# A hybrid encoder layer: the output norm of cross attention with its roots on ScalarE and VectorE, later first-half rows, other PSUM banks and five early FFN pairs

## The chip, the cores and the metric

The kernel runs on one core of one Trainium2 chip. The core has five engines with a queue each, worked off in order: TensorE (PE, matmuls and transposes), VectorE (DVE), ScalarE (ACT), GpSimd (POOL) and SyncE (SP), whose queue issues the DMAs here. The metric is the device time of one execution in microseconds (us).

## The reference

One layer of an encoder trunk in float32, for 1024 tokens of width 1024. Three sub-layers follow each other, each inside two RMS norms, one ahead of it and one on its output before it is added to the residual stream:

```python
c = _memory_cross_attention(_rms_norm(x, g_cross_pre[l]), _rms_norm(mem, g_mem[l]),
                            w_cq[l], w_ckv[l], w_co[l])
x = x + _rms_norm(c, g_cross_post[l])
f = _swiglu(_rms_norm(x, g_ffn_pre[l]), w_gate_up[l], w_down[l])
x = x + _rms_norm(f, g_ffn_post[l])
```

`_rms_norm(x, g)` is `x * rsqrt(mean(x*x) + EPS) * g` along a row, `_swiglu` is `(silu(h @ w_gate) * (h @ w_up)) @ w_down` with 2816 columns each for gate and up. The mixer ahead of this (attention and a delta rule) is not touched.

## The kernel before, in words

Every float32 product is made of three matmuls: each operand is split into a high part `hi` (a cast on ACT) and a low part `lo` (the difference, on DVE or POOL), and hi·hi, hi·lo and lo·hi are summed in PSUM. `split` (line 100) issues the two instructions (lines 103 and 104, or 106 and 107 where a gain is multiplied in). `load_w` (line 119) brings a weight matrix of 128x1024 into one of two buffers `wraw`, and splits it into one of two pairs `whi`, `wlo`. A `wraw` buffer is free again when its `lo` has been computed, a `whi`, `wlo` pair when its last matmul has run.

The stretch around the change comes in this order:

1. The output projection of cross attention (lines 1277 to 1412) is a Strassen-like product of 2x2 blocks. Its last two products are issued by tile of 128 rows (`by_tile`, line 1385), on four PSUM banks `X`, two of the pool `PN` and two of `PX`. After each tile `then(t)` follows: `second_rows(t)` for rows 4 to 7 of eight (tokens 512 to 1023, tensor `zl`), and in the last product `first_half_rows(t)` for rows 0 to 3 (tensor `zz`).
2. `row_end` (line 1391) and `finish` (line 1308) end a row: square and sum its second half (ACT), multiply by the gain `gp` (`gained`), the reciprocal root of the mean square, scale and add the residual (line 1315), store to `d_x2` (line 1316), then square and sum again (line 1318), a second reciprocal root (lines 161 and 162), and scale for the FFN's input norm (line 1322 on ACT for even rows, line 1324 on DVE for odd rows). Each root is `(s + c)` to the power -0.5 on POOL, line 1314 or 162.
3. The rows are turned. `turned_k` (line 1418) makes four transposes of 128x128 into one bank. The eight blocks `k` of rows 4 to 7 come first (line 1430), each split into `x1h`, `x1l`; blocks 0 to 3 are the operand `X11`, blocks 4 to 7 `X21`. Then the blocks of rows 0 to 3 are turned, and combined with the first into `T1` to `T4` and `X22` (lines 1438 to 1455), mostly on DVE.
4. The FFN's gate and up matrices are worked in 11 pairs of 256 columns. For the first `EARLY` pairs (loop at line 1474) the products with `X11` and `X21`, which need only rows 4 to 7, are made ahead, while rows 0 to 3 and `T1` to `T4` still come into being: for each of two matrices 12 matmuls with `X11`, a copy to `d_m1` (line 1483), 12 matmuls with `X21`, then SiLU (line 1487), a product (line 1488) and a store to `d_a`. That is 48 matmuls to a pair, on four banks `PG`, two to a pair.
5. The main loop (line 1564) takes all 11 pairs, early and other pairs in turn. `pair_weights` (line 1507) loads each pair's matrices (for early pairs a second time), sums their blocks on POOL and DVE (lines 1516 to 1519) and splits the sums. An early pair reads `d_m1` and `d_a` back and has 48 matmuls fewer here. The first matmuls are `pB`, with `T2`.

What sets the order: the program is traced as written, and a scheduler then lays out each engine's queue with a simulation of time; of what is ready in that simulation, what was traced first goes first. `tc.high_priority(AHEAD)` counts an instruction as traced 300 earlier. `tc.issue_after(i)` puts the instructions of its block that run on `i`'s engine behind `i` in that engine's queue; it adds no wait and binds no other engine.

Of the kernel before, what the change touches and what calls it, by code (L numbers as in the profile page):

```python
# [10 lines left out]
F32 = mybir.dt.float32  # L11
F32R = mybir.dt.float32r
I32 = mybir.dt.int32
AF = mybir.ActivationFunctionType
ALU = mybir.AluOpType
# [4 lines left out]
P = 128  # L20
S = 1024
D = 1024
# [4 lines left out]
EPS = 1e-6  # L27
# [1 line left out]
AHEAD = 300  # L29
ML = 256  # L30

EARLY = 4

# [41 lines left out]
def tile_hybrid_block(  # L77
# [6 lines left out]
    nc = tc.nc  # L84
# [9 lines left out]
    def f32(ap):  # L94
        return ap.bitcast(F32)
# [4 lines left out]
    def split(hi, lo, src, scale=None, eng=None):  # L100

        if scale is None:
            nc.scalar.copy(hi, src)  # L103
            (eng or nc.vector).tensor_tensor(lo, src, f32(hi), ALU.subtract)  # L104
        else:
            nc.scalar.activation(hi, src, AF.Identity, scale=scale)
            nc.vector.scalar_tensor_tensor(lo, src, scale, f32(hi), ALU.mult, ALU.subtract)

    def pool(name, bufs, **kw):
        return tc.tile_pool(name=name, bufs=bufs, reuse_waits="tile", **kw)  # L110

    cst = ctx.enter_context(pool("cst", 1))
# [20 lines left out]
    ident = cst.tile([P, P], F32, name="ident")  # L133
    mhalf = cst.tile([P, 16], F32, name="mhalf")
    nc.gpsimd.memset(mhalf, -0.5)
    cols = cst.tile([P, P], F32, name="cols")
    p12 = ExitStack()
    sm = p12.enter_context(pool("sm", 1))
# [19 lines left out]
    def rstd_of(rs, ss, n, eps):  # L158

        w = ss.shape[-1]  # L160
        nc.gpsimd.tensor_scalar(rs, ss, n, eps, ALU.mult, ALU.add)
        nc.gpsimd.tensor_tensor(rs, rs, mhalf[:, :w], ALU.pow)
# [5 lines left out]
    def gain(n, k):  # L168
        return cols[:, gain_at[n] + k:gain_at[n] + k + 1]
# [28 lines left out]
    def small():  # L198
        return ps.tile([P, 512], F32, tag="ps", name="ps")
# [11 lines left out]
    for hf in range(2):  # L211
        hi = hx.tile([P, KT, HALF], F32R, name=f"hhi{hf}")
        lo = hx.tile([P, KT, HALF], F32R, name=f"hlo{hf}")
        for j in range(4):
            t = 4 * hf + j
# [4 lines left out]
            ss = t1.tile([P, 1], F32, tag="ss", name="ss", bufs=4)  # L220
            nc.scalar.activation(junk, xt, AF.Square, accum_out=ss)
            rs = t1.tile([P, 1], F32, tag="rs", name="rs", bufs=4)
            rstd_of(rs, ss, 1.0 / D, EPS)
            nc.vector.scalar_tensor_tensor(xt, xt, rs, gmix, ALU.mult, ALU.mult)
            for kq in range(2):
                pt = small()
# [15 lines left out]
    pt = small()  # L242
# [75 lines left out]
    pt = small()  # L318
# [42 lines left out]
    pt = small()  # L361
# [640 lines left out]
    HK = KT // 2  # L1002
# [19 lines left out]
    def operand(pool_, tag):  # L1022
        if tag == "s1":
            return [Halves(opB, b0), Halves(opB3, "b3")]
        if tag == "s0":
            return [Halves(opA, f"s0{c}") for c in "hl"]
        if tag in places:
            return [p_.tile([P, KT, HALF], F32R, tag=t, name=t) for p_, t in places[tag]]
        return [pool_.tile([P, KT, HALF], F32R, tag=f"{tag}{i}", name=f"{tag}{i}") for i in range(2)]
# [20 lines left out]
    PG, PN, PX = (pg, "pg"), (pn, "pn"), (px, "px")  # L1050
# [198 lines left out]
    zl = opC.tile([P, 4, D], F32, tag="x22", name="zl")  # L1249
# [3 lines left out]
    zz = tz.tile([P, 4, D], F32, name="zz")  # L1253
    zv, za = zl[:, :, 0:HALF], zl[:, :, HALF:]
    ssq = tz.tile([P, 2, NT], F32, name="ssq")

    def blocks(t):
        return t[:, 0:HK], t[:, HK:KT]
# [45 lines left out]
    def square_of(src, ch, r):  # L1304
        jk = tz.tile([P, HALF], F32, tag="junk", name="junk")
        nc.scalar.activation(jk, src, AF.Square, accum_out=ssq[:, ch, r:r + 1])

    def finish(r, z, eng):

        tok = slice(r * P, (r + 1) * P)  # L1310
        xr = res[r]
        rs = tz.tile([P, 1], F32, tag="prs", name="prs", bufs=4)
        nc.vector.tensor_scalar(rs, ssq[:, 1, r:r + 1], ssq[:, 0, r:r + 1], D * EPS, ALU.add, ALU.add)
        nc.gpsimd.tensor_tensor(rs, rs, mhalf[:, 0:1], ALU.pow)
        nc.vector.scalar_tensor_tensor(xr, z, rs, xr, ALU.mult, ALU.add)
        nc.sync.dma_start(d_x2[tok, :], xr)
        s2 = tz.tile([P, 1], F32, tag="ps2", name="ps2", bufs=4)
        nc.scalar.activation(z, xr, AF.Square, accum_out=s2)
        r2 = tz.tile([P, 1], F32, tag="pr2", name="pr2", bufs=4)
        rstd_of(r2, s2, 1.0 / D, EPS)  # L1320
        if eng is nc.scalar:
            nc.scalar.activation(z, xr, AF.Identity, scale=r2)
        else:
            nc.vector.tensor_scalar(z, xr, r2, None, ALU.mult)

    a11, a12, s3_, a22 = ((q_[0][:, c], q_[1][:, c]) for q_ in (q0, q1) for c in (slice(0, HK), slice(HK, KT)))
    s1_, s4_ = ([r_, [t[:, c] for t in q1]] for r_, c in zip(blocks(raw), (slice(HK, KT), slice(0, HK))))
# [4 lines left out]
    def add(o_, a, b_):  # L1332
        nc.vector.tensor_tensor(o_, a, b_, ALU.add)

    def gained(o_, src, c_, eng=nc.gpsimd):
        eng.tensor_tensor(o_, src, gp[:, c_], ALU.mult)

    LO, HI = slice(0, HALF), slice(HALF, D)
# [22 lines left out]
    for t in range(4):  # L1361
        add(zv[:, t], zv[:, t], X[t])
        square_of(zv[:, t], 0, 4 + t)
        gained(zv[:, t], zv[:, t], LO)

    def residual_row(r, place=None):
        if place is None:
# [23 lines left out]
    def row_end(z, r):  # L1391
        square_of(z[:, HI], 1, r)
        gained(z[:, HI], z[:, HI], HI, nc.vector)
        finish(r, z, (nc.scalar, nc.vector)[r % 2])

    def second_rows(t):
        add(za[:, t], y7[:, t], X[t])
        row_end(zl[:, t], 4 + t)

    def first_half_rows(t):  # L1400
        add(zz[:, t, HI], e_[:, t], X[t])
        row_end(zz[:, t], t)

    by_tile([act_part(s1_, k) for k in (0, 2)], resident(1, ("s0h1", "s0l0")), False, second_rows)
    two_rows(0, "s0h1")
    two_rows(2, "s0h0")
# [8 lines left out]
    x1h, x1l = operand(opB, "s1")  # L1415
    X11, X21 = (x1h[:, 0:HK], x1l[:, 0:HK]), (x1h[:, HK:KT], x1l[:, HK:KT])

    def turned_k(parts, k, at=PN):
        pt = at[0].tile([P, 512], F32, tag=at[1], name="ptn")
        for j in range(4):  # L1420
            nc.tensor.transpose(pt[:, j * P:(j + 1) * P], parts(j, k), ident)
        return pt
# [5 lines left out]
        return zz[:, j, k * P:(k + 1) * P]  # L1428

    for k in range(KT):  # L1430
        pt = turned_k(first_rows, k, (PN, PX)[k % 2])
        split(x1h[:, k, :], x1l[:, k, :], pt, gain("ffn", k))
        nc.gpsimd.tensor_tensor(raw[:, k, :], f32(x1h[:, k, :]), f32(x1l[:, k, :]), ALU.add)
    tr = LR2.enter_context(pool("tr", 1, side="right"))
    T2, T4 = (blocks(t) for t in operand(opA, "s0"))
    T1, T3 = (blocks(t) for t in operand(opB, "s2"))
# [23 lines left out]
    d_a = {n: dram.tile([NB, P, HALF], F32, name=f"d_a{n}") for n in ("11", "12", "22", "s1", "s2", "s3", "s4")}  # L1460
    d_m1 = dram.tile([2 * EARLY, P, HALF], F32, name="d_m1")

# [9 lines left out]
    te = LP.enter_context(pool("te", 2, side="right"))  # L1472
    for e in range(EARLY):
        f = 2 * e
# [31 lines left out]
    def pair_weights(c0, early):  # L1506

        with tc.high_priority(AHEAD):
            raws = []
            for i in range(2):  # L1510
                raws.append(wp.tile([P, KT, P], F32, tag="wraw", name="wraw"))
                load = nc.sync.dma_start(raws[i], w_gate_up[:, c0 + i * P:c0 + (i + 1) * P].rearrange("(k p) n -> p k n", p=P))
            a_, b_ = raws
            s = [ws.tile([P, HK, P], F32, tag="sr", name="sr", bufs=3) for _ in range(4)]
            hl = {i: [ws.tile([P, HK, P], F32R, tag=f"s{i}{c}", name=f"s{i}{c}") for c in "hl"] for i in (1, 0, 2, 3)}
            nc.gpsimd.tensor_tensor(s[0], b_[:, 0:HK], b_[:, HK:], ALU.add)  # L1516
            nc.vector.tensor_tensor(s[1], s[0], a_[:, 0:HK], ALU.subtract)
            nc.gpsimd.tensor_tensor(s[2], a_[:, 0:HK], b_[:, 0:HK], ALU.subtract)
            nc.vector.tensor_tensor(s[3], a_[:, HK:], s[1], ALU.subtract)
            for i in (1, 0, 2, 3):  # L1520
                split(*hl[i], s[i])
            W1 = None
            if not early:
                ahi = wp.tile([P, KT, P], F32R, tag="whi", name="whi")
                alo = wp.tile([P, KT, P], F32R, tag="wlo", name="wlo")
                split(ahi, alo, a_, eng=nc.gpsimd)
                W1 = (ahi[:, 0:HK], alo[:, 0:HK]), (ahi[:, HK:], alo[:, HK:])
            W22 = [tg.tile([P, HK, P], F32R, tag=n, name=n) for n in ("bhi", "blo")]
            split(*W22, b_[:, HK:])
        return W1, W22, [hl[i] for i in range(4)], load  # L1530
# [28 lines left out]

    turns = [p for e in range(EARLY) for p in (e, EARLY + e)] + list(range(2 * EARLY, NB))  # L1560
    for f in (2 * p for p in turns):
        early = f // 2 < EARLY
        wts = [pair_weights(c0, early) for c0 in (f * P, FF + f * P)]
# [35 lines left out]
        s1, s2 = (tg.tile([P, HALF], F32, tag="sa", name="sa") for _ in range(2))  # L1599
# [29 lines left out]
    zz = keep.tile([P, 4, D], F32, name="zz")  # L1629
    za, zv = (keep.tile([P, 4, 512], F32, name=n) for n in ("za", "zv"))  # L1630
# [113 lines left out]
    for t in range(4):  # L1744
# [13 lines left out]
        r = 4 + t  # L1758
        xr = residual(r)
# [4 lines left out]
        rs = rstd_at(r)  # L1764
# [35 lines left out]
```

## Time and profile before

| | |
|---|---|
| median of three runs | 1534.2 us (1531.57 to 1537.82) |
| the profiled execution | 1537.92 us, its span 1536.2 us |
| mean granted TensorE clock | 0.992 |
| DVE busy | 1109.5 us (72%), 1790 instructions |
| ACT busy | 742.3 us (48%), 1516 instructions |
| POOL busy | 396.3 us (26%), 404 instructions |
| HBM | 166 GB/s over the span |

How to read the lines that follow. A timeline row gives the start, the duration, the engine, the source line, the operation with its output and inputs, the count, and in brackets the idle time before it and who ended it. Rows of several instructions are merged: the duration runs to the end of the last. Matmuls are pipelined: each is shown with about 0.39 us, though one starts every 0.23 us, so the rate is read from starts. A windows row gives a stretch, its length, each engine's busy time with its instruction count, the granted TensorE clock (1.00 is full), the DMA share and GB/s. A row of groups gives line, engine, operation, shapes and count, then busy us and mean ns of one.

### The profile page before, as it was taken

Reading aid. Unit: us, or ns where it says so; the run is one execution under the profiler, and the core shown is the slowest. Engines: PE = TensorE matmul, PEld = TensorE weight load, DVE = VectorE, ACT = ScalarE, POOL = GpSimd, SP = SyncE. Lnnn points to the kernel's source line nnn. Section 1 sums busy time; section 2 is a strip of 40 time slices with the busy share of each in tenths; the row PEclk is TensorE's granted clock in tenths of the full one; section 3 lists DMA queues with packets and bytes.
Section 4 is the critical chain, followed back from the end, with each engine's and each line's share of the span. In section 5 each row is a group of like instructions: output and inputs, shape, how many; then the busy total and the mean of one; then the engine's idle time right before and its main releaser. Section 6 shows DMA issues by size and latency. Waiting matters only on the chain.

```text
span 1536.2 us, 21190 instructions
## 1 busy us (share of the span) xinstructions
PE 1477.0 (96%) x7403; PEld 1241.1 (81%) x7403; DVE 1109.5 (72%) x1790; ACT 742.3 (48%) x1516; POOL 396.3 (26%) x404
## 2 busy tenths in 40 slices
PE   6999999999999999999999898999999999999997
PEld 5888878878899778887888686888888888888786
DVE  6868999787888865538466876676877555696665
ACT  5678821447557764456454663323223332454532
POOL 2020221311326203242201622343443332000021
PEclk9999999999999999999999999999999999999999
DMA  6235575856987684457725534343533333863354
GB/s 207 76 105 151 144 194 152 218 161 181 317 285 233 196 284 155 152 160 261 236 89 185 192 129 125 124 131 110 172 123 102 104 103 103 317 214 95 106 176 166
DMA packets 272360, 258.70 MB, mean 168 GB/s; under 512 B 34793, under 2 KB 204670, under 8 KB 272254
## 3 DMA queue, kind: packets, MB, share of 16 engines
q1 hardware_dynamic: 272253, 257.35, 53.3%
q8 instruction: 58, 0.95, 0.3%
q14 instruction: 49, 0.39, 0.1%
HBM read 179.41 MB, written 75.27 MB: 166 GB/s over the span
## 4 chain that ended last, share of the span: by engine, by line
PE 70%; DVE 11%; DMA 8%; ACT 6%; issue 3%; SPq 1%; POOL 1%; DVEq 0%; POOLq 0%; ACTq 0%
PE pE L1466 8%; PE pD L1466 8%; PE pA L1466 7%; PE pg L261 6%; PE pmg L1070 6%; PE pdX L1657 6%; PE pcq L261 4%; PE pdA L1657 4%; PE pB L1466 4%; PE pst L1286 3%; PE psc L809 2%; PE pdX L1754 2%; PE pdD L1657 2%; DVE acc L286 2%; DMA wraw<-in_w_ckv_dram 1%
## 5 line engine op out<-in xcount | busy, mean ns | idle before, releaser
L103 ACT CAST whi<-wraw 128x1024 fp32r<-128x1024 f32 x96 | 100.9, 1052 | 142.6 <-DMA wraw<-in_w_gate_up_dram 29.5
L104 POOL TENSOR_TENSOR wlo<-wraw,whi 128x1024 fp32r<-128x1024 f32 x38 | 91.9, 2419 | 188.9 <-ACT whi L103 180.2
L261 PE MATMUL pg<-hlo,whi 128*128 128x512 f32 x352 | 139.5, 397 | 0.0
L261 PE MATMUL pg<-hhi,whi 128*128 128x512 f32 x352 | 139.2, 396 | 0.0
L261 PE MATMUL pg<-hhi,wlo 128*128 128x512 f32 x352 | 138.4, 394 | 0.0
L1466 PE MATMUL pA<-b,whi 128*128 128x512 f32 x352 | 113.1, 402 | 5.9 <-ACT m L1483 3.4
L104 DVE TENSOR_TENSOR wlo<-wraw,whi 128x1024 fp32r<-128x1024 f32 x58 | 73.7, 1272 | 42.2 <-ACT whi L103 39.7
L1466 PEld LDWEIGHTS pA<-b,whi 128*128 128x128 f32 x352 | 67.4, 193 | 20.3 <-ACT m L1483 3.8
L1657 PE MATMUL pdX<-dhl,whi 128*128 128x512 f32 x264 | 76.1, 391 | 1.5 <-ACT dhl L103 0.8
L261 PEld LDWEIGHTS pg<-hhi,whi 128*128 128x128 f32 x352 | 66.5, 189 | 13.3 <-ACT hhi L103 0.2
L261 PEld LDWEIGHTS pg<-hhi,wlo 128*128 128x128 f32 x352 | 66.5, 189 | 12.8
L261 PEld LDWEIGHTS pg<-hlo,whi 128*128 128x128 f32 x352 | 66.4, 189 | 12.7
L1544 POOL TENSOR_TENSOR act<-act,up 128x512 f32<-128x512 f32 x33 | 49.5, 1501 | 95.9 <-DVE up L1543 62.6
L1466 PE MATMUL pA<-b,wlo 128*128 128x512 f32 x176 | 69.9, 398 | 0.0
L103 ACT CAST whi<-araw 128x1024 fp32r<-128x1024 f32 (+1 forms) x36 | 35.3, 981 | 67.7 <-PE pdX L1657 24.4
L104 DVE TENSOR_TENSOR wlo<-araw,whi 128x1024 fp32r<-128x1024 f32 (+1 forms) x36 | 40.8, 1134 | 35.0 <-ACT whi L103 34.9
L1516 POOL TENSOR_TENSOR sr<-wraw 128x512 f32<-128x512 f32 x22 | 30.0, 1366 | 130.4 <-DMA wraw<-in_w_gate_up_dram 119.1
L286 DVE SCALAR_TENSOR_TENSOR acc<-cp,cols,acc 128x1024 f32<-128x1024 f32 x48 | 62.1, 1295 | 0.1
L1691 POOL TENSOR_SCALAR frs<-sq 128x1 f32<-128x1 f32 x8 | 11.9, 1496 | 193.6 <-ACT jk L1676 192.7
L1657 PEld LDWEIGHTS pdX<-dhl,whi 128*128 128x128 f32 x264 | 49.3, 188 | 12.8 <-ACT dhl L103 1.1
L1466 PE MATMUL pB<-s0h,s1h 128*128 128x512 f32 x176 | 54.4, 391 | 3.4 <-ACT s1h L103 3.4
L103 ACT CAST dhl<-b 128x512 fp32r<-128x512 f32 x66 | 40.3, 620 | 31.6 <-PE pdA L1657 13.7
(481 smaller groups left out, 4302.2 us busy)
## 6 DMA issues: line engine op xcount, KB each, us to landing
wraw<-in_w_gate_up_dram SPq DMA_DIRECT2D x52, 512.0 KB, 3.9
kv<-d_kv SPq DMA_DIRECT2D x32, 512.0 KB, 6.8
wraw<-in_w_in_dram SPq DMA_DIRECT2D x22, 512.0 KB, 4.2
b<-in_w_down_dram SPq DMA_DIRECT2D x20, 512.0 KB, 7.7
araw<-d_as SPq DMA_DIRECT2D x20, 512.0 KB, 3.7
pz<-d_pz SPq DMA_DIRECT2D x32, 256.0 KB, 7.3
wraw<-in_w_ckv_dram SPq DMA_DIRECT2D x16, 512.0 KB, 5.1
wraw<-in_w_out_dram SPq DMA_DIRECT2D x16, 512.0 KB, 3.7
```

The lines of the kernel that those rows point to most:

```text
L103: nc.scalar.copy(hi, src)
L104: (eng or nc.vector).tensor_tensor(lo, src, f32(hi), ALU.subtract)
L261: nc.tensor.matmul(p_, w[:, k, :], ah[a][:, k, :], start=(k == 0 and i == 0), stop=(k == nk - 1 and i == 2))
L286: nc.vector.scalar_tensor_tensor(acc, cp[:, t:t + S], taps[t], acc, ALU.mult, ALU.add)
L809: nc.tensor.matmul(out[:, d, h, :], lt[:, d, h, :], rt[:, d, h, :], start=True, stop=True)
L1070: nc.tensor.matmul(pp[t], act[a][:, k, tt], w_[:, kk, :], start=(k == 0 and i == 0), stop=(k == KT - 1 and i == 2))
L1286: nc.tensor.matmul(bank, a[:, tt], w, start=(start and i == 0), stop=(stop and i == 2), skip_group_check=not check)
L1466: nc.tensor.matmul(out_, w[a][:, k, :], xx[b_][:, k, :], start=(start and k == 0 and i == 0), stop=(k == HK - 1 and i == 2), skip_group_ch ...
L1516: nc.gpsimd.tensor_tensor(s[0], b_[:, 0:HK], b_[:, HK:], ALU.add)
L1544: nc.gpsimd.tensor_tensor(o_, o_, up, ALU.mult)
L1657: nc.tensor.matmul(banks[t], a[:, k - k0, tt], w, start=(first and k == 0 and i == 0), stop=(k == NB - 1 and i == 2), skip_group_check=not ...
L1754: nc.tensor.matmul(X[t], a[:, k], w[:, k0 + k], start=False, stop=(k0 + k == NB - 1 and i == 2), skip_group_check=True)
```

## The change

Six edits, all in the kernel between the cross attention and the FFN:

- Both roots of `finish` become `inverse_root`: Sqrt on ACT with the constant as its bias, then a reciprocal on DVE. The constant of the first root is now added once to the sums `ssq[:, 0]` (one small DVE instruction), and `epsc` holds that of the second (one memset on POOL at the start).
- The scaling at a row's end goes to DVE for rows 4 to 7 and to ACT for rows 0 to 3; before it went by even and odd.
- The gain on the first halves of rows 4 to 7 goes from POOL to DVE.
- `row_end` of rows 0 to 3 is traced later: behind the split of block 3 of rows 4 to 7, its DVE instructions queued behind that split's; before it came in `first_half_rows`.
- Blocks 0 to 3 of rows 4 to 7 are turned into `PG` banks in place of `PN` and `PX`.
- `EARLY` is 5 in place of 4.

```diff
-EARLY = 4
+EARLY = 5
...
         if scale is None:
             nc.scalar.copy(hi, src)
-            (eng or nc.vector).tensor_tensor(lo, src, f32(hi), ALU.subtract)
-        else:
-            nc.scalar.activation(hi, src, AF.Identity, scale=scale)
-            nc.vector.scalar_tensor_tensor(lo, src, scale, f32(hi), ALU.mult, ALU.subtract)
+            return (eng or nc.vector).tensor_tensor(lo, src, f32(hi), ALU.subtract)
+        nc.scalar.activation(hi, src, AF.Identity, scale=scale)
+        return nc.vector.scalar_tensor_tensor(lo, src, scale, f32(hi), ALU.mult, ALU.subtract)
...
+    epsc = cst.tile([P, 1], F32, name="epsc")
+    nc.gpsimd.memset(epsc, EPS)
...
+    def inverse_root(rs, ss, scale, bias):
+        nc.scalar.activation(rs, ss, AF.Sqrt, bias=bias, scale=scale)
+        nc.vector.reciprocal(rs, rs)
+
     def finish(r, z, eng):
...
-        nc.vector.tensor_scalar(rs, ssq[:, 1, r:r + 1], ssq[:, 0, r:r + 1], D * EPS, ALU.add, ALU.add)
-        nc.gpsimd.tensor_tensor(rs, rs, mhalf[:, 0:1], ALU.pow)
+        inverse_root(rs, ssq[:, 1, r:r + 1], 1.0, ssq[:, 0, r:r + 1])
...
-        rstd_of(r2, s2, 1.0 / D, EPS)
+        inverse_root(r2, s2, 1.0 / D, epsc)
         if eng is nc.scalar:
-            nc.scalar.activation(z, xr, AF.Identity, scale=r2)
-        else:
-            nc.vector.tensor_scalar(z, xr, r2, None, ALU.mult)
+            return nc.scalar.activation(z, xr, AF.Identity, scale=r2)
+        return nc.vector.tensor_scalar(z, xr, r2, None, ALU.mult)
...
-        gained(zv[:, t], zv[:, t], LO)
+        gained(zv[:, t], zv[:, t], LO, nc.vector)
+    nc.vector.tensor_scalar(ssq[:, 0], ssq[:, 0], D * EPS, None, ALU.add)
...
     def row_end(z, r):
         square_of(z[:, HI], 1, r)
         gained(z[:, HI], z[:, HI], HI, nc.vector)
-        finish(r, z, (nc.scalar, nc.vector)[r % 2])
+        return finish(r, z, nc.vector if r >= 4 else nc.scalar)
+
+    scaled = []
 
     def second_rows(t):
         add(za[:, t], y7[:, t], X[t])
-        row_end(zl[:, t], 4 + t)
+        scaled.append(row_end(zl[:, t], 4 + t))
 
     def first_half_rows(t):
         add(zz[:, t, HI], e_[:, t], X[t])
-        row_end(zz[:, t], t)
...
     for k in range(KT):
-        pt = turned_k(first_rows, k, (PN, PX)[k % 2])
-        split(x1h[:, k, :], x1l[:, k, :], pt, gain("ffn", k))
+        pt = turned_k(first_rows, k, PG if k < HK else (PN, PX)[k % 2])
+        cut = split(x1h[:, k, :], x1l[:, k, :], pt, gain("ffn", k))
         nc.gpsimd.tensor_tensor(raw[:, k, :], f32(x1h[:, k, :]), f32(x1l[:, k, :]), ALU.add)
+        if k == HK - 1:
+            with tc.issue_after(cut.ins):
+                for t in range(4):
+                    row_end(zz[:, t], t)
```

## The prediction

> **What bounds the kernel now.** I read the page's busy times first, then windows around the changed lines, then each engine's timeline there.
>
> ```profile
> PE 1477.0 (96%) x7403; PEld 1241.1 (81%) x7403; DVE 1109.5 (72%) x1790; ACT 742.3 (48%) x1516; POOL 396.3 (26%) x404
> ...
> 848.00:859.70 11.70, 11.70 (x53) 9.72 (x52) 10.21 (x13) 6.86 (x17) 8.13 (x7) 1.00 0.35 114
> ...
> 870.70:878.10 7.40, 2.49 (x17) 1.54 (x15) 6.47 (x10) 5.42 (x13) 4.75 (x7) 0.84 0.44 177
> 878.10:886.10 8.00, 7.21 (x20) 5.48 (x21) 6.17 (x10) 5.59 (x10) 7.13 (x8) 0.50 0.33 131
> ...
> 894.10:928.70 34.60, 34.60 (x167) 28.73 (x165) 29.99 (x43) 24.09 (x39) 0.00 (x0) 1.00 0.52 164
> 928.70:932.40 3.70, 0.35 (x2) 0.00 (x0) 2.31 (x4) 1.95 (x4) 1.10 (x1) 1.00 0.12 37
> 932.40:938.70 6.30, 4.32 (x12) 2.89 (x12) 2.61 (x5) 1.24 (x3) 1.86 (x2) 0.73 0.18 63
> ...
> 947.20:948.60 1.40, 0.04 (x2) 0.03 (x1) 1.36 (x3) 0.70 (x2) 0.12 (x1) 1.00 0.05 15
> ...
> 1080.00:1120.00 40.00, 40.00 (x179) 33.11 (x178) 33.03 (x39) 11.80 (x20) 17.54 (x11) 1.00 0.44 142
> ```
>
> PE is the bound: full in the projection (848), among the early pairs (894) and in the main loop (1080). So only what lets PE stand, or slows its clock, can be won, and two places hold that. At the first, where rows 4 to 7 are turned, PE idles 7.40 - 2.49 = 4.91 us, then 8.00 - 7.21 = 0.79, and works 7.21 us at half clock, a loss of 3.6: together 9.3. At the second, where the main loop begins, it idles 3.70 - 0.35 = 3.35, 6.30 - 4.32 = 1.98 and 1.40 - 0.04 = 1.36, and 4.32 us at 0.73 lose 1.2: together 7.9. All there is to win is 17.2 us.
>
> ```profile
> 859.74 11.04 PE L1286 MATMUL pst<-part,b 128*128 128x512 f32 x48
> 870.63 0.81 PE L1421 MATMUL ptn<-ident,zl 128*128 128x128 f32 x6
> 872.50 0.44 PE L1421 MATMUL ptn<-ident,zl 128*128 128x128 f32 x2 [1.06 <-DVE zl L1324]
> ...
> 874.89 0.66 PE L1421 MATMUL ptn<-ident,zl 128*128 128x128 f32 x4 [1.14 <-DVE zz L1333]
> 878.10 1.22 PE L1466 MATMUL pA<-b,whi 128*128 128x512 f32 x2 [2.56 <-ACT b L106]
> ...
> 907.26 1.04 PE L1421 MATMUL ptn<-ident,zz 128*128 128x128 f32 x8
> 908.05 0.48 PE L1466 MATMUL pA<-b,wlo 128*128 128x512 f32 x1
> ...
> 932.41 0.73 PE L1466 MATMUL pA<-b,whi 128*128 128x512 f32 x2 [3.35 <-ACT m L1483]
> ```
>
> The first place has three waits: for row 7's scaling (L1324), for a bank that `first_half_rows` still reads (L1333), and for block 0's cast (L106), which stood in ACT's queue behind rows 0 to 3. The rates are here too: 48 matmuls in 870.63 - 859.74 = 10.9 us, which is one early pair, and 8 transposes in 908.05 - 907.26 = 0.8 us.
>
> **Roots, scaling and gain: when are rows 4 to 7 ready?**
>
> ```profile
> 865.80 1.28 DVE L1315 SCALAR_TENSOR_TENSOR xr<-zl,prs,xr 128x1024 f32<-128x1024 f32 x1
> 867.00 0.69 DVE L1336 TENSOR_TENSOR zz<-zz,gpost 128x512 f32<-128x512 f32 x1
> 867.60 0.21 DVE L1313 TENSOR_SCALAR prs<-ssq 128x1 f32<-128x1 f32 x1
> ...
> 871.70 0.74 DVE L1324 TENSOR_SCALAR zl<-xr,pr 128x1024 f32<-128x1024 f32 x1
> ...
> 866.05 2.04 POOL L162 TENSOR_TENSOR pr<-pr,mhalf 128x1 f32<-128x1 f32 x1
> ...
> 868.13 1.16 ACT L1322 ACTIVATE zl<-xr,pr 128x1024 f32<-128x1024 f32 x1 [1.42 <-POOL pr L162]
> 869.18 1.04 ACT L1318 ACTIVATE zl<-xr 128x1024 f32<-128x1024 f32 x1
> 870.13 0.18 ACT L1318 ACTIVATION_READ_ACCUMULATOR zl<-xr 128x1 f32 x1
> ...
> L667 ACT ACTIVATE es<-es 128x4 f32<-128x4 f32 x16 | 3.2, 198 | 10.9 <-POOL es L666 10.9
> L371 ACT ACTIVATE EG<-ps 128x12 f32<-128x12 f32 x8 | 0.7, 236 | 0.0
> L1168 DVE RECIPROCAL csum<-csum 128x2 f32<-128x2 f32 x16 | 2.5, 159 | 1.9 <-ACT cpr L1166 1.9
> ```
>
> Row 7's residual is added by 867.08, but its square starts only at 869.18: ACT stood at row 6's scaling, which waited for a POOL power of 2.04 us. After the change that scaling is DVE's and the power is gone. The trace has no Sqrt; the smallest activations bound it by 0.20 and 0.24 us (I take 0.24, since the bias is one operand more), and a reciprocal is 0.16. So the square ends at 867.1 + 1.1 + 0.2 = 868.4, root and reciprocal at 868.8, the scaling of 0.74 at about 869.6. The reciprocals are new waits of DVE on ACT, with the next row's gain and residual add queued behind each; they cost the 0.24 of a root where ACT is free, and up to a square more (1.04) where it is not. The gain, no longer POOL's, costs DVE four times 0.69 around 850; it and two more scalings of 0.74 are paid by the DVE work of rows 0 and 1 that leaves this stretch (0.69, 1.28 and 0.21 a row). PE's own product ends at 870.7, so this lies in its shadow with a microsecond to spare. The memset and the sum over `ssq` are single small instructions off every chain.
>
> ```profile
> 893.14 1.05 ACT L103 CAST whi<-wraw 128x1024 fp32r<-128x1024 f32 x1 [2.38 <-PE pA L1466]
> 894.21 1.28 ACT L1487 ACT_TABLE_LOAD   x1
> 895.51 0.60 ACT L1487 ACTIVATE sg<-pA 128x512 f32<-128x512 f32 x1
> ```
>
> Sqrt needs a table load of its own, as SiLU does here: 1.28 us, once, before row 4's first root, where ACT has time (6.86 busy of 11.70 in the row at 848). Were Sqrt and the first SiLU to alternate, each switch would add 1.28; with rows 0 to 3 rooted before 890 and the first pair's SiLU behind its 24 last matmuls, I expect none. [...]
>
> **Banks and later rows: the first early pair.**
>
> ```profile
> 877.38 2.39 ACT L106 ACTIVATE b<-ptn,cols 128x512 fp32r<-128x512 f32 x4
> ...
> 879.31 2.06 DVE L107 SCALAR_TENSOR_TENSOR b<-ptn,cols,b 128x512 fp32r<-128x512 f32 x3
> ```
>
> With `PG` banks long free, 16 transposes start at 870.7 and take 1.6 us. Block 0's cast (0.6) and low part (0.7) end at 872.7, so PE waits some 0.4 us in place of the 4.91 and 0.79, and keeps its clock. DVE splits blocks 0 to 3 until 874.7 (0.67 each). Then come the row ends, traced before blocks 4 to 7: on DVE gain 0.60 (867.00 to 867.60), two reciprocals of 0.13 (the spacing of such small instructions, 867.60 to the next at 867.73) and the residual add 1.20 (865.80 to 867.00), some 2.05 a row, four rows until 882.9. Only then the low parts of blocks 4 to 7, the first at 883.6. PE meanwhile has 16 transposes (1.6) and 24 matmuls with `X11` (5.45), until 879.8. So **a new hole** of 3.8 us opens before `X21`, and after the like hole of 3.35 us the clock cost 1.2. Bounds: nothing, if the low parts slip in between the rows; 9 us and more, if ACT's casts are stuck too (rival C). I take the middle, 5.0 with the clock, because program order decides between ready instructions. The first place then loses 0.4 + 5.0 in place of 9.3: 3.9 won.
>
> [...]
>
> The four stores to `d_x2` move in SP's queue too; the next load behind them, the third early pair's, came only at 895.48, so nothing waits for them.
>
> **The fifth early pair: where the main loop begins.**
>
> ```profile
> 895.48 0.38 SPq L126 DMA_DIRECT2D wraw<-in_w_gate_up_dram  x1
> ...
> 925.16 0.38 SPq L1512 DMA_DIRECT2D wraw<-in_w_gate_up_dram  x1
> ...
> 920.19 1.06 ACT L103 CAST whi<-wraw 128x1024 fp32r<-128x1024 f32 x1
> ...
> 931.25 0.62 ACT L103 CAST bhi<-wraw 128x512 fp32r<-128x512 f32 x1 [1.71 <-DMA wraw<-in_w_gate_up_dram]
> 931.78 0.58 ACT L1483 COPY m<-pA 128x512 f32<-128x512 f32 x1
> ...
> 923.38 1.22 DVE L104 TENSOR_TENSOR wlo<-wraw,whi 128x1024 fp32r<-128x1024 f32 x1
> ...
> 936.76 0.69 DVE L1488 TENSOR_TENSOR sg<-sg,pA 128x512 f32<-128x512 f32 x1 [3.65 <-PE pA L1466]
> ```
>
> The stall of 3.35 us: the copy `m` stands in ACT's queue behind a cast that waits for a weight. That weight was issued at 925.16, when the last early `wlo` had freed its buffer; and `wlo` came 2.1 us after its cast (921.25 to 923.38), because DVE, 29.99 busy of 34.60, was behind with `T1` to `T4`. Five pairs give PE 10.9 us more to do here, and the main loop, full of PE work, gets 10.9 less: by itself that moves work and wins nothing. But DVE's remaining work grows by only two low parts of 1.22 and a product of 0.69, so it has caught up when the fifth pair starts, and the weight comes 2 to 3 us sooner against PE. I take the stall of 3.35 and its clock loss of 1.2 as gone (4.5) and the other two, 1.98 and 1.36, as kept: `pB` waits for a sum that stands on DVE behind `sg`, which is itself queued for PE's last early matmul. The bounds are nothing and 7.9. The fifth pair's weights are loaded twice; DMA is at 0.52 and 0.44 of its time here and in the loop, so that is covered.
>
> **Sum.** 3.9 + 4.5 = 8.4 us. Against the profiled execution, span 1536.2 and 1537.92 with what lies around it, that gives 1529.5. That execution stands 3.7 above the median of the runs; from the median the same saving gives 1525.8, and I say 1526.
>
> **The rivals.**
> - A: no hole, because DVE's gaps take the low parts of blocks 4 to 7 (in the old trace DVE did slip three low parts, at 879.31, in among the row ends). Then 5.0 more is won: 13.4, that is 1521; with the last two stalls gone as well, 1517.
> - B: the start of the main loop stalls as before, since the first weight must still wait for the last early pair's buffer, whichever pair that is. Only the 3.9 remain: 1530.
> - C, slower: on ACT, too, the ends of rows 0 to 3 stand ahead of the casts of blocks 4 to 7. A row there is a square (1.04 + 0.18), two roots (0.48) and a scaling (1.16), 2.9 us; behind the first residual add at 876.7, four rows end at 888.3. PE then idles 879.8 to 889, 9.2 us, and pays the half clock of 3.6 again: 13.2 with the 0.4, against 9.3 before, so 3.9 lost. If the rows go one behind the other, with DVE's 2.05 in each, four take 19.8 us from 874.7: `X21` at 895, and 19.2 lost against 9.3. With B's stalls kept: 1538 to 1544. It decides from the point where block 4's cast starts later than about 885. For it speaks the program order; against it, that ACT has gaps here (5.59 busy of 8.00 at 878) and that the first casts of the old trace got in among the rows.
>
> **How the numbers follow.** My forecast gets 0.42, A 0.30, B 0.12, C 0.16. The range 1517 to 1539 holds A whole, the forecast, B and the mild end of C. Half a per cent, about what a measurement of this kernel can tell from no change, is 7.7 us: faster means below 1526.5, slower above 1541.9. The forecast lies at the border, so a little over half of it (0.22) and all of A count as faster, 0.52; the rest of the forecast (0.20), B and 0.02 of C as same, 0.34; 0.14 of C as slower.
>
> **What would show it.** Right: transposes of block 0 directly behind the projection, no wait for L1333, `pA` from about 873 at full clock; then a hole near 880 that ends with a low part of line 107; one table load for Sqrt and one for SiLU; at the last early pair, `m` no longer behind a cast that waits for a weight. Wrong: row 7 ready after 871; PE waiting for a cast of line 106 near 880 (C); Sqrt and SiLU loads alternating; 3 us or more idle again where the main loop begins; PE idle in the loop itself.

## The result, and the profile after

| | median us | lowest to highest | runs |
|---|---|---|---|
| before | 1533.05 | 1530.78 to 1538.32 | 6 |
| after | 1547.11 | 1543.41 to 1551.06 | 6 |

The ratio is 1.0076, with the 95% interval 1.0057 to 1.0095: the changed kernel is slower by about 0.8%, some 12 us. The profiled execution took 1548.03 us, its span is 1546.3. Forecast were 1526 and a range that ended at 1539.

The place where the time went isn't the stretch that was changed. The busy times of the changed kernel's page, to be held against PE 1477.0 before:

```profile
PE 1491.9 (96%) x7403; PEld 1240.7 (80%) x7403; DVE 1120.2 (72%) x1805; ACT 749.5 (48%) x1535; POOL 373.7 (24%) x375
```

PE runs the same 7403 matmuls and is busy 14.9 us longer with them. A window deep in the main loop, where PE never stands and has its full clock in both, says the same; the columns after the length are the busy time and the number of instructions of PE, weight loads, DVE, ACT and POOL, then the clock, the DMA share and GB/s. Before:

```profile
1000.00:1300.00 300.00, 300.00 (x1326) 248.49 (x1325) 205.42 (x248) 86.92 (x139) 116.37 (x72) 1.00 0.37 120
```

After:

```profile
1000.00:1300.00 300.00, 300.00 (x1295) 242.63 (x1295) 214.87 (x256) 86.38 (x141) 114.58 (x71) 1.00 0.39 126
```

1295 matmuls in place of 1326, in 300 us without a gap. So one matmul takes longer, and the view of the loop's line, which lists minimum, median and maximum in ns for each group, tells which. Before:

```profile
L1466 PE MATMUL pB<-s0h,s1h x176: 388/390/500, 938.8 to 1294.1; 128*128 128x512 f32 x176
...
L1466 PE MATMUL pE<-b,s2h x176: 388/389/390, 942.1 to 1299.5; 128*128 128x512 f32 x176
...
L1466 PE MATMUL pE<-s0l,bhi x176: 388/389/390, 960.0 to 1315.8; 128*128 128x512 f32 x176
```

After:

```profile
L1475 PE MATMUL pB<-s0h,s1h x176: 387/389/499, 951.3 to 1303.2; 128*128 128x512 f32 x176
...
L1475 PE MATMUL pE<-b,s2h x176: 393/395/397, 956.2 to 1308.8; 128*128 128x512 f32 x176
...
L1475 PE MATMUL pE<-s0l,bhi x176: 392/396/397, 972.5 to 1325.5; 128*128 128x512 f32 x176
```

`pB` is as it was, `pE` takes some 6 ns more in every one of its matmuls: the minima of after, 393 and 392, lie above the maximum of before, 390. The code says what parts the two. A pool lies either on the left of SBUF or, with `side="right"`, on the right. `pB` multiplies `T2` (in `opA`, right) by weights in `ws` (right). `pE<-b,s2h` multiplies `T3` (in `opB`, left) by `ws` (right), and `pE<-s0l,bhi` multiplies `T4` (`opA`, right) by `bhi` in `tg` (left). Slower are the products whose two operands lie on opposite sides. In the main loop these are all of `pD` and `pE`: 22 halves of a pair, 4 products of 12 matmuls in each, 1056 in all. The one edit of the diff that moves one side against the other is the smallest: `epsc`, a 128x1 tile in `cst` on the left. It is taken here as 32 bytes of each partition, so that every left tile behind it lies 32 bytes farther up; e5 below, where 32 bytes go from the right and the group is back at 390 ns, bears that out.

The loop isn't the only place with such products. Ahead of the stretch, in the output projection, `pst<-tw,b` multiplies rows in `opB` (left) by `tw` in `opA` (right). Before, then after:

```profile
L1286 PE MATMUL pst<-tw,b x96: 388/389/390, 827.6 to 859.5; 128*128 128x512 f32 x96
...
L1287 PE MATMUL pst<-tw,b x96: 395/396/397, 830.5 to 863.4; 128*128 128x512 f32 x96
```

In the changed stretch itself the profile looks as follows. PE's timeline of after (start, length, then the idle time before and what ended it):

```profile
874.54 3.66 PE L1426 MATMUL ptn<-ident,zl 128*128 128x128 f32 x32
878.19 0.73 PE L1475 MATMUL pA<-b,whi 128*128 128x512 f32 x2
...
886.14 0.50 PE L1475 MATMUL pA<-b,whi 128*128 128x512 f32 x1 [1.51 <-DVE b L106]
...
896.55 0.50 PE L1475 MATMUL pA<-b,wlo 128*128 128x512 f32 x1 [2.08 <-DVE wlo L104]
...
944.43 0.73 PE L1475 MATMUL pA<-b,whi 128*128 128x512 f32 x2 [0.72 <-ACT m L1492]
...
951.34 0.73 PE L1475 MATMUL pB<-s0h,s1h 128*128 128x512 f32 x2 [3.89 <-ACT s1h L103]
```

And the windows over it:

```profile
880.00:890.00 10.00, 8.27 (x30) 6.12 (x29) 10.00 (x15) 3.70 (x8) 7.99 (x6) 0.86 0.21 79
890.00:900.00 10.00, 7.47 (x25) 5.39 (x24) 8.48 (x8) 8.62 (x12) 4.21 (x2) 0.84 0.69 244
900.00:940.00 40.00, 39.53 (x187) 32.28 (x187) 30.48 (x46) 31.23 (x49) 0.00 (x0) 0.99 0.49 157
940.00:950.00 10.00, 6.74 (x28) 4.59 (x26) 5.36 (x7) 2.43 (x4) 2.99 (x2) 1.00 0.41 133
950.00:960.00 10.00, 8.66 (x31) 6.95 (x32) 6.19 (x8) 3.97 (x7) 2.99 (x2) 0.83 0.41 114
```

The 32 transposes follow the projection without a gap, and the early pair follows them without one: the waits of 4.91 and 0.79 us and the half clock under them are gone. Idle time and slowed clock, summed as in the prediction (idle plus busy times the missing clock), are 2.9, 3.7, 0.9, 3.3 and 2.8 us in the five rows, 13.6 together, against 17.2 before. So the stretch gained 3.6 us while the kernel lost 12.

The waits that are left start on DVE. Its timeline, after:

```profile
881.30 1.70 DVE L1339 TENSOR_TENSOR zz<-zz,gpost 128x512 f32<-128x512 f32 x1
...
884.70 0.67 DVE L1339 TENSOR_TENSOR zz<-zz,gpost 128x512 f32<-128x512 f32 x1
...
887.33 1.27 DVE L1319 SCALAR_TENSOR_TENSOR xr<-zz,prs,xr 128x1024 f32<-128x1024 f32 x1
...
889.18 6.11 DVE L1319 SCALAR_TENSOR_TENSOR xr<-zz,prs,xr 128x1024 f32<-128x1024 f32 x3
...
895.29 1.20 DVE L104 TENSOR_TENSOR wlo<-wraw,whi 128x1024 fp32r<-128x1024 f32 x1
...
947.50 0.69 DVE L1497 TENSOR_TENSOR sg<-sg,pA 128x512 f32<-128x512 f32 x1 [0.82 <-PE pA L1475]
948.10 0.68 DVE L1526 TENSOR_TENSOR sr<-sr,wraw 128x512 f32<-128x512 f32 x1
```

POOL's, at the same time:

```profile
878.22 5.94 POOL L1438 TENSOR_TENSOR oraw<-b,b 128x512 f32<-128x512 f32 x4 [31.70 <-DVE b L106]
886.17 8.04 POOL L1438 TENSOR_TENSOR oraw<-b,b 128x512 f32<-128x512 f32 x4 [2.02 <-DVE b L106]
```

While POOL adds `oraw`, a gain takes 1.70 us on DVE in place of the 0.67 at 884.70, where POOL stands. Of the residual adds the first, at 887.33, began just ahead of POOL's second addition there (887.42 in the trace) and kept its 1.27; the three behind it took 2.04 on average (6.11 together). The rows 0 to 3 were moved into exactly that time. The low part `wlo` of the second early pair stands behind the three adds, and PE waits 2.08 us for it. Beside POOL's additions the rows here give 1.0 us more for such a gain (1.70 against 0.67) and 0.8 on average for a residual add (2.04 against 1.27); what holds the operations up isn't shown.

ACT's timeline, after:

```profile
858.28 1.28 ACT L1310 ACT_TABLE_LOAD   x1
...
893.70 1.28 ACT L1496 ACT_TABLE_LOAD   x1
894.99 0.60 ACT L1496 ACTIVATE sg<-pA 128x512 f32<-128x512 f32 x1
895.60 1.28 ACT L1310 ACT_TABLE_LOAD   x1
896.90 0.29 ACT L1310 ACTIVATE pr<-ps,epsc 128x1 f32<-128x1 f32 x1
...
907.49 1.28 ACT L1496 ACT_TABLE_LOAD   x1
...
950.67 0.62 ACT L103 CAST s1h<-sr 128x512 fp32r<-128x512 f32 x1 [3.89 <-DMA d_a<-sg]
```

Sqrt and SiLU do alternate, with four loads of 1.28 us here in place of the one before. Behind each load the activation starts 0.01 to 0.02 us later.

### The profile page after: what moved, and what is told of

Its sections match the earlier page's. It is cut to its first block, busy times and chain, and to the rows that moved or that the text cites. A ratio compares the mean times of both kernels' runs of the same rounds, so it can differ in the third digit from the quotient of the medians.

```text
span 1546.3 us, 21213 instructions
## 1 busy us (share of the span) xinstructions
PE 1491.9 (96%) x7403; PEld 1240.7 (80%) x7403; DVE 1120.2 (72%) x1805; ACT 749.5 (48%) x1535; POOL 373.7 (24%) x375
## 4 chain that ended last, share of the span: by engine, by line
PE 64%; DVE 10%; DMA 8%; ACT 4%; issue 3%; SPq 1%; POOL 1%; DVEq 0%; POOLq 0%; ACTq 0%
PE pD L1475 8%; PE pE L1475 8%; PE pA L1475 7%; PE pmg L1071 6%; PE pdX L1666 6%; PE pst L1287 5%; PE pcq L262 4%; PE pB L1475 4%; PE pdA L1666 2%; PE psc L810 2%; PE pdX L1763 2%; PE pdD L1666 2%; DMA wraw<-in_w_ckv_dram 2%; PE pco L1186 1%; DMA kv<-d_kv 1%
## 5 line engine op out<-in xcount | busy, mean ns | idle before, releaser
L104 POOL TENSOR_TENSOR wlo<-wraw,whi 128x1024 fp32r<-128x1024 f32 x36 | 87.3, 2426 | 187.0 <-ACT whi L103 177.1
L262 PEld LDWEIGHTS pg<-hhi,whi 128*128 128x128 f32 x352 | 66.4, 189 | 14.9 <-ACT hhi L103 0.2
L1475 PE MATMUL pD<-b,s0h 128*128 128x512 f32 x176 | 56.6, 402 | 0.0
```

Of the source, the lines that this page charges most:

```text
L104: return (eng or nc.vector).tensor_tensor(lo, src, f32(hi), ALU.subtract)
L262: nc.tensor.matmul(p_, w[:, k, :], ah[a][:, k, :], start=(k == 0 and i == 0), stop=(k == nk - 1 and i == 2))
L1475: nc.tensor.matmul(out_, w[a][:, k, :], xx[b_][:, k, :], start=(start and k == 0 and i == 0), stop=(k == HK - 1 and i == 2), skip_group_ch ...
```

## The experiments

Theory D (distance; the expectations of e1 to e4 call it S, for shift): the 32 bytes of `epsc` slow the matmuls of mixed sides, that is with one operand on the left and one on the right, and without them the changed kernel is some us faster than before. Rival Q (queues): another order of instructions or other waits cost the time, and the slower matmuls are a by-product of a fuller DVE or more DMA. The runs named e and g3 part the two; f and the other g ask what the scheduling edits are worth.

**The constant in the old pad (e1).** The kernel holds a tile `off` of 128x8, 32 bytes on the right side, which nothing reads. The changed kernel, with `epsc` as a column of it:

```diff
-    nc.gpsimd.memset(off.tile([P, 8], F32, name="off"), 0.0)
+    offt = off.tile([P, 8], F32, name="off")
+    nc.gpsimd.memset(offt, 0.0)
...
-    epsc = cst.tile([P, 1], F32, name="epsc")
+    epsc = offt[:, 0:1]
```

> The changed kernel, but the constant epsc lies in the first column of the pad tile on the right side that is there anyway, so that no tile on the left side moves; the order of the instructions stays. Theory S (the new tile of 32 bytes shifts every left-side tile against the right-side ones, and each matmul with one operand on either side starts 6 ns later; some 2,700 such matmuls of 512 columns, 16 us): 1530 to 1534 us, and the group pE<-b,s2h is back from 395 to 389 ns. Theory Q (the loss lies in the stretch of the change: two more table switches, residual adds of 2 us, a wait of 3.9 us before pB): 1545 to 1549 us, 395 ns unchanged or irrelevant.

Measured: ratio to before 0.9983 (0.9969 to 0.9998), median 1534.94. Its groups, and two rows of its timeline of PE:

```profile
L1476 PE MATMUL pB<-s0h,s1h x176: 389/389/690, 948.3 to 1292.3; 128*128 128x512 f32 x176
...
L1476 PE MATMUL pE<-b,s2h x176: 389/389/393, 953.2 to 1297.8; 128*128 128x512 f32 x176
...
L1476 PE MATMUL pE<-s0l,bhi x176: 389/389/389, 969.1 to 1314.1; 128*128 128x512 f32 x176
```

```profile
871.68 3.65 PE L1427 MATMUL ptn<-ident,zl 128*128 128x128 f32 x32
...
948.33 1.12 PE L1476 MATMUL pB<-s0h,s1h 128*128 128x512 f32 x2 [3.79 <-ACT s1h L103]
```

All mixed groups are back at 389, with every edit of the schedule still there. The two spans, 1546.3 and 1535.1, differ by 11.2 us, and these rows say where. From the first `pE<-b,s2h` to the last `pE<-s0l,bhi`: 1325.5 - 956.2 = 369.3 against 1314.1 - 953.2 = 360.9, that is 8.4, or 8 ns for each of the 1056 mixed matmuls of the loop from one start to the next. From the transposes to the first `pB`: 76.80 against 76.65, nothing. So the larger part of the loss lies outside the changed stretch, in the loop. The other 2.9 us (874.54 - 871.68) lie ahead of the transposes. Mixed groups such as `pst<-tw,b` are slower there too, but how much of the 2.9 is theirs isn't shown: among kernels with the old distance the profiled executions reach the transposes anywhere from 865.67 (f1) to 873.44 (f2).

**The shift alone, in the kernel before (e2), and twice of it (e3).** A tile that nothing reads, of 32 or of 64 bytes:

```diff
+    epsc = cst.tile([P, 1], F32, name="epsc")
+    nc.gpsimd.memset(epsc, EPS)
```

```diff
+    epsc = cst.tile([P, 16], F32, name="epsc")
+    nc.gpsimd.memset(epsc, EPS)
```

> The kernel before, plus only the tile epsc (128x1, padded to 32 bytes) on the left side and its memset; nothing reads it. Theory S: 1547 to 1550 us, pE<-b,s2h 395 ns, pE or pst groups with both operands on one side still 389. Theory Q: 1533 us, as before, since no queue changes.

> The kernel before, plus an unread tile of 64 bytes in place of 32. Theory S, if the rule is the address difference of the two operands modulo 64 bytes: 1533 us and 389 ns again. If any shift away from the old addresses costs: 1547 to 1550 us. Theory Q: 1533 us, so this run only tells the two forms of S apart, together with the run of 32 bytes.

Measured: e2 1.0081 (1.0064 to 1.0098); e3 1.003 (1.0018 to 1.0042). The group of e2:

```profile
L1468 PE MATMUL pE<-b,s2h x176: 392/395/397, 945.5 to 1309.8; 128*128 128x512 f32 x176
```

and of e3:

```profile
L1468 PE MATMUL pE<-b,s2h x176: 388/392/397, 944.5 to 1305.1; 128*128 128x512 f32 x176
```

e2 has none of the change but its 32 bytes, and loses all that the change loses. In its profile every engine runs the instructions of before in the order of before, and POOL one memset more. So Q falls. 64 bytes are neither as good as none nor as bad as 32: about half of the group, 87 of 176 matmuls in e3's trace, takes 388 ns and runs undisturbed.

**The distance from the other side (e4, e5, g3).** If the distance counts and not the address, the pad on the right must do what the tile on the left does. e4 is the changed kernel with a pad of 64 bytes:

```diff
-    nc.gpsimd.memset(off.tile([P, 8], F32, name="off"), 0.0)
+    nc.gpsimd.memset(off.tile([P, 16], F32, name="off"), 0.0)
```

e5 is the changed kernel without the pad, and g3 the kernel before without it:

```diff
-    nc.gpsimd.memset(off.tile([P, 8], F32, name="off"), 0.0)
```

> The changed kernel with its tile epsc where it is, but the pad tile on the right side is 64 bytes in place of 32, so that the right side moves by 32 bytes too; every queue has the same instructions in the same order. Theory S in the form that only the difference between the sides counts: 1530 to 1534 us, as with epsc in the pad. If the left side's own address counts: 1547 us. Theory Q: 1547 us.

> The changed kernel with its tile epsc on the left, but without the pad tile on the right side: now both sides lie 32 bytes away from where they lay in the kernel before, and the distance between them is the old one. Theory D (only the distance between the two operands of a matmul counts): every group back to 389 ns, as with epsc in the pad, ratio to the kernel before 0.997 to 1.000. If a side's own address counts: 395 ns stays, ratio 1.006 to 1.008.

> The kernel before without the pad of 32 bytes on the right side that nothing reads: the two sides then lie 32 bytes apart from where they lie in the kernel before, in the other direction than with one more 32-byte tile on the left as seen from either side it is the same shift of 32 bytes. If only the size of the distance counts: matmuls of mixed sides (pE<-b,s2h) at 392/395 as in the kernel with the shift of 32, ratio 1.007 to 1.009. Rival: the pad is there for something else and its removal changes nothing: 388/389, ratio 1.000.

Measured: e4 1.0058 (1.0041 to 1.0076), e5 0.9996 (0.9985 to 1.0006), g3 1.0083 (1.0058 to 1.0108). Their groups, e4's first:

```profile
L1475 PE MATMUL pE<-b,s2h x176: 388/392/397, 956.6 to 1306.0; 128*128 128x512 f32 x176
```

then e5's:

```profile
L1473 PE MATMUL pE<-b,s2h x176: 388/390/390, 949.8 to 1294.3; 128*128 128x512 f32 x176
```

then g3's:

```profile
L1465 PE MATMUL pE<-b,s2h x176: 395/396/397, 939.8 to 1303.8; 128*128 128x512 f32 x176
```

The expectation of e4 had the sign of its pad wrong. If left tiles are laid from one end and right tiles from the other, a pad on the right brings the sides closer, as a tile on the left does; then e4 stands at 64 bytes like e3, and e5 at the old distance. This reading was made after the result of e4, but before e5 ran, and e5 bears it out. With it the medians of all eight kernels fall in place by the distance alone, counted from the kernel before. The last column is the time from the first to the last start of the group, out of the rows above, less PE's idle time in it (1.36 in before, 0.18 in e2, none in the others). Before, e2, e3 and g3 have four early pairs and the others five, so only kernels of one kind are held against each other:

| distance of the sides | kernels | median of `pE<-b,s2h`, ns | ratio to before | first to last start, us |
|---|---|---|---|---|
| 32 bytes wider | g3 | 396 | 1.0083 | 364.0 |
| as before | before, e1, e5 | 389, 389, 390 | 1, 0.9983, 0.9996 | 356.0, 344.6, 344.5 |
| 32 closer | after, e2 | 395, 395 | 1.0076, 1.0081 | 352.6, 364.1 |
| 64 closer | e3, e4 | 392, 392 | 1.003, 1.0058 | 360.6, 349.4 |

Against the old distance the loop loses 8.0 (g3), 8.0 (after) and 8.1 us (e2) at 32 bytes, and 4.6 (e3) and 4.8 (e4) at 64. In the time of the whole kernel e4 loses more than e3; that difference lies outside the loop. One part of it shows in the profiles: from the first transposes to the first `pB` e3 takes 65.1 us, before 68.1. Why e3 waits less there was not looked into.

g3 adds and moves no instruction: in the profile each engine keeps the order of before. It takes a memset away and slows the kernel by 0.8%. The pad that nothing reads held the kernel at the good distance. And the shift of 32 bytes cost about the same in either direction, whether a tile was added (1.0081) or taken away (1.0083).

**What the schedule is worth (f1, f2, f3).** All three start from e1, so that no shift hides what they do. f1 has four early pairs again:

```diff
-EARLY = 5
+EARLY = 4
```

f2 has both roots by POOL's power, the second by `rstd_of` as before:

```diff
-        inverse_root(rs, ssq[:, 1, r:r + 1], 1.0, ssq[:, 0, r:r + 1])
+        nc.vector.tensor_scalar(rs, ssq[:, 1, r:r + 1], ssq[:, 0, r:r + 1], D * EPS, ALU.add, ALU.add)
+        nc.gpsimd.tensor_tensor(rs, rs, mhalf[:, 0:1], ALU.pow)
...
-        inverse_root(r2, s2, 1.0 / D, epsc)
+        rstd_of(r2, s2, 1.0 / D, EPS)
...
-    nc.vector.tensor_scalar(ssq[:, 0], ssq[:, 0], D * EPS, None, ALU.add)
```

f3 has the row ends of rows 0 to 3 behind the last block of rows 4 to 7:

```diff
-        if k == HK - 1:
+        if k == KT - 1:
```

> The changed kernel with epsc in the pad tile (no shift), and EARLY back at 4. Theory E (the fifth pair covers the late T1 to T4): pB then waits for T2 some 5 to 8 us, ratio to the kernel before 1.002 to 1.004. Theory W (with an odd number of early pairs the cast s1h waits for the last pair's store of sg, whose buffer it takes, 1.7 us, which just eats what the pair covers): the wait of s1h for the DMA d_a<-sg is gone, and the ratio is that of five pairs, 0.997 to 0.999.

> The changed kernel with epsc in the pad tile (no shift), but both roots on POOL again; banks, order, scaling engines and five pairs as changed. Theory R (the roots on ACT are what makes rows 4 to 7 ready in time): the first transposes wait 2 to 3 us again, ratio 1.000 to 1.002. Theory T (the two extra table switches and the roots among the casts cost as much as they bring): the waits of PE near 880 and 893 shrink by 2 to 3 us, ratio 0.996 to 0.998.

> The changed kernel with epsc in the pad tile (no shift), the row ends of rows 0 to 3 traced behind block 7 in place of block 3. Theory H (they open the hole before X21): the wait of PE for DVE L106 of 1.5 us and its half clock are gone, 3 us, ratio 0.995 to 0.997. Rival: T1 to T4 come later by as much, and the wait before pB grows from 3.8 to 6 us or more: ratio 0.998 to 1.000.

Measured: f1 1.0007 (0.9995 to 1.0019), f2 0.9995 (0.9979 to 1.001), f3 0.9987 (0.9973 to 1.0). The intervals of f2 and f3 hold most of e1's; f1's meets it only at its end (0.9995 against 0.9998), so the fifth pair may be worth some 0.2%. The waits show what each does. The first `pB` of f1:

```profile
933.27 1.22 PE L1476 MATMUL pB<-s0h,s1h 128*128 128x512 f32 x2 [6.43 <-ACT s1h L103]
```

With four pairs DVE is still at `T1` to `T4` when the loop begins, and PE waits 6.4 us in place of 3.8: the fifth pair does give DVE its time. This is theory E's wait, with less loss than it expected. Of theory W only the wait for the store is gone (f1's `s1h` waits for DVE); what stands in its place is longer. f2's transposes, and the start of its second early pair:

```profile
873.44 3.65 PE L1427 MATMUL ptn<-ident,zl 128*128 128x128 f32 x32
...
893.46 0.73 PE L1476 MATMUL pA<-b,whi 128*128 128x512 f32 x2 [1.45 <-ACT whi L103]
895.90 0.80 PE L1476 MATMUL pA<-b,wlo 128*128 128x512 f32 x1 [1.70 <-DVE wlo L104]
```

The transposes run in one piece, with no wait ahead of them, though both roots are on POOL again: theory R falls. The same two waits as in after stand at the second pair, 3.15 us in sum against 2.08 + 0.45, so without the loads for Sqrt PE waits no less, and theory T falls too. What the place of the roots is worth lies within the intervals. f3:

```profile
889.06 1.22 PE L1476 MATMUL pA<-b,whi 128*128 128x512 f32 x2 [5.84 <-ACT whi L103]
```

The hole ahead of `X21` is closed and a wait of 5.84 us for a weight's cast opened: it moved. The wait ahead of the first `pB` stayed at 3.81, so the rival's mechanism didn't come either.

**Six early pairs (g1), and with f3's rows (g2).** In e1 and in after, the first `s1h` of the loop waits for a store: the sum is there at 948.78 (948.10 + 0.68), but the cast starts at 950.67, and its row names the transfer `d_a<-sg`, which reads the last pair's product out of a buffer on the right. With an even number of pairs the buffers fall otherwise.

```diff
-EARLY = 5
+EARLY = 6
...
-    turns = [p for e in range(EARLY) for p in (e, EARLY + e)] + list(range(2 * EARLY, NB))
+    turns = [p for e in range(EARLY) for p in (e, EARLY + e) if p < NB]
```

> The kernel e1 (the changed kernel with its constant in the old pad, so that no tile is shifted) with six early pairs in place of five; the early pairs and the others take turns in the main loop until they run out. Theory: with an even number of pairs the first s1h of the main loop takes a buffer that no store still reads, as with four, and VectorE has finished with T1 to T4 before the last early pair, as with five; so TensorE's wait ahead of the first pB (3.8 us with five, 6.4 with four) falls to 2 us or less, and the time to about 1533. Rival: sixteen more stores and loads and an early pair that ends in the same chain of SiLU, product and sum leave the wait at 3 to 4 us, since only the chain counts: time as e1, 1535.

> The kernel f3 (e1 with the row ends of rows 0 to 3 queued behind the last block) with six early pairs. Theory: the row ends of rows 0 to 3 and then T1 to T4 come later on VectorE than in e1, and six pairs give them 10.9 us more of TensorE's work to hide under; the hole ahead of X21 stays closed and the wait ahead of the first pB is short: 1530 to 1532, the fastest of all. Rival: T1 to T4 are hidden anyway with five, and the wait of 5.8 us for a weight's cast stays: 1533, as f3.

Measured: g1 0.9995 (0.9982 to 1.0009), g2 0.9994 (0.9981 to 1.0007). g1's timeline of PE:

```profile
950.43 0.73 PE L1476 MATMUL pA<-b,whi 128*128 128x512 f32 x2 [1.88 <-ACT m L1493]
...
957.07 0.73 PE L1476 MATMUL pB<-s0h,s1h 128*128 128x512 f32 x2 [2.03 <-ACT s1h L103]
```

The wait ahead of `pB` falls from 3.8 to 2.0 as expected, and the stall behind `m`, 0.72 with five pairs, is back with 1.88. The sum of the two is 3.9 in place of e1's 4.5, and the time doesn't show it: in the same execution the two waits at the start of the second pair are 1.38 + 2.74, where e1 has 0.46 + 2.08. In g2 the wait for the weight's cast stays (5.76), as its rival said, and it isn't the fastest. Of all that was run, e1 is the fastest against before, with an interval that just leaves out no change.

## Why the prediction was wrong

**The step that failed** is the sentence "The memset and the sum over `ssq` are single small instructions off every chain." As instructions they are. But `epsc` is also a tile, and its 32 bytes change the distance of all left tiles to all right ones; e2, with nothing but them, costs 1.0081, the whole of the change's 1.0076. The sum had no term for a tile's place, and none of the rivals had one: C, the slower one, ended at 1538 to 1544 by a mechanism that didn't come (the casts of blocks 4 to 7 were not stuck on ACT). "What would show it wrong" had no sign for it either: PE idle in the loop was named, PE slower in the loop was not. Two of the signs that it named did come, the alternating loads and an idle time of 3 us or more where the main loop begins (3.89), but neither is where the time went.

**The first place** was to lose 5.4 us in place of 9.3. It loses 2.9 + 3.7 = 6.6 in the rows at 880 and 890. Right: no wait for L1333, `pA` behind the transposes, full clock, row 7 ready in PE's shadow (873.73, 0.8 us before the projection ends at 874.54; all of this execution is some 4 us later here than the profile of before, so the sign "row 7 ready after 871" says nothing). A Sqrt is 0.29 us, taken as 0.24. The expected hole ahead of `X21` is there and ends with a low part of L106 (107 before), but with 1.51 us and not 3.8: three low parts slipped in between the gains and the residual adds, which was rival A's mechanism in part. What was not costed is the second wait, 2.08 us for `wlo`, and the reason of it: the residual adds were taken at 1.20 each from the row at 865.80, where the add had begun ahead of POOL's power and kept its 1.28, while the power, begun at 866.05, took 2.04. Behind POOL's `oraw` three of them took 2.04.

The same reading touches the roots. The power of 2.04 us that held row 6 lay beside DVE's add and gain; begun while DVE stood, the same power in the kernel before takes 0.55, so by the author's estimate the other 1.5 us were a wait for DVE:

```profile
870.68 0.55 POOL L162 TENSOR_TENSOR pr<-pr,mhalf 128x1 f32<-128x1 f32 x1
```

That fits f2, where the powers came back and no transpose waited.

**The clock** cost 1.2 us in the row of the hole (8.27 busy at 0.86), as taken, and again in the next row (7.47 busy at 0.84). The longest waits of PE in these two rows are 1.51 and 2.08 us; the 0.73 of before stood behind 3.35. How long a hole must be to cost clock isn't shown.

**The table loads** were expected once each; there are four, because the second roots of rows 1 to 3 came after the first pair's SiLU, and not before 890. That they hurt little is f2's result. Beside its 1.28 us a load shows no further time in the trace: the cast ahead of it ends at 893.68, 893.70 + 1.28 is 894.98, and the SiLU starts at 894.99.

**The second place** was to lose 3.3 us in place of 7.9. The rows at 940 and 950 lose 3.3 + 2.8 = 6.1. The stall behind `m` shrank from 3.35 to 0.72, as said. Of the other two, taken as kept, the 1.36 is gone, but the 1.98 ahead of the first `pB` became 3.89. Its mechanism, a sum on DVE behind `sg`, was one half of it: the sum is there at 948.78; the other half is the buffer that the store of `sg` still holds until the cast at 950.67. Rival B, stalls as before, was wrong in its cause and nearer in its price than the forecast (7.9 and 3.3 against the 6.1).

**The sum.** The edits of the schedule won 3.6 us in the stretch and not 8.4. In the time of the kernel, e1 puts them at 0.17% or 2.6 us (0.3 to 4.8), e5 at 0.04% (a loss of 0.9 to a gain of 2.3). So their size came out at less than half of the forecast, and even their direction is barely shown: e1's interval just leaves out no change, e5's holds it. Against them stand some 12 us for 32 bytes.

## What to carry to other kernels

When a kernel gains or loses a small tile, compare the matmuls' minimum and median per group with those before, ahead of any reading of waits: a rate that changes in groups far from the edit, while their engine never stands, may be a matter of memory layout, as it was here (395 ns in place of 389). A pad that nothing reads may be holding a layout; try a new constant in it, or move the pad along. And an operation moved to DVE is costed from a row in which POOL did what it will do at the new place, and had begun first (here 2.04 us an add, where 1.20 was taken).

## What the runs showed of the hardware

In these runs the time of a 512-column matmul of fp32r with one operand on each side changed with the distance of the sides in SBUF. The medians of `pE<-b,s2h` are 389 and 390 ns with the sides as in before, 395 and 396 when they are shifted by 32 bytes to either side, 392 at 64 (one direction tried). From start to start that is some 8 ns in the main loop at 32 bytes. All pairs of tiles of a group were shifted together; the distances of single pairs were not read out. Why, and how it goes on at other distances, was not tried.
